# Group A attention: halo queries copied from wider q tiles, v stored by head group, one store for the halo outputs

## The chip, the cores and the metric

The kernel runs on one core of one Trainium2 chip. The metric is device time in microseconds for one launch; the program has float32 inputs and outputs. The engines are named as in the profile: PE (TensorE, matmul), PEld (its weight loads), DVE (VectorE), ACT (ScalarE), POOL (GpSimd) and SP (SyncE), which here only issues DMAs. A DMA that SP or ACT issues is followed by its queue: an engine issues its instructions in order, and an instruction whose wait is not over holds up those behind it.

## What is computed

One encoder layer with shared weights runs on two inputs, a prompt of 1024 tokens (sequence 0) and a sample of 512 tokens (sequence 1). Sixteen meta tokens are put before each, so n is 1040 and 528.

```python
n = rms_norm(x, g_mix)
qa, ka, va, qb, kb, vb = split(n @ w_in)
# group A: 8 query heads of 64, 2 key/value heads (4 query heads share one), per-head RMS norm of q and k, rotary
oa = softmax(qa @ ka.T * scale) @ va
# group B: 4 heads, each with two softmax maps, the second weighted by a learned lambda and subtracted
ob = rms_norm((softmax(q1 @ k1.T * scale) - lam * softmax(q2 @ k2.T * scale)) @ vb)
h = x + concat(oa, ob) @ w_out
# ConvGLU: depthwise convolution of width 3 over positions, GELU, gate
h = h + (gelu(conv3(rms_norm(h) @ w_gate)) * (rms_norm(h) @ w_up)) @ w_down
y = rms_norm(h)[16:]
```

The convolution of the first token that is returned (position 16) needs the row of position 15. Of the sixteen meta queries, position 15 alone is therefore computed: this is the halo.

## The kernel before

Matmuls that need float32 accuracy are done with a high part and a low part of each operand: `split` writes the high part on ACT and the rest on DVE or POOL, and `mm3` multiplies three times.

`projection` makes q, k and v for one sequence and stores them in DRAM. `pair` and `keys_a` write q and k as `qk` and `ka`; `values` writes v. For group A (`j == VA`) v in DRAM was `[128 tokens, n // 128 blocks, 256]`: for each token the high and low parts of key/value head 0 (128 columns), then those of head 1.

`attention` reads them back. For group A it loops over two key/value heads (`kv`), the four query heads of each (`i`), and blocks of 512 queries (`b`; two blocks for the prompt, one for the sample). `load_k` and `load_v` run once per `kv`; `load_q` runs once per block and loads two tiles `q0` and `q1` (high and low stacked in both orders) of 128 rows each, from a DRAM view whose outermost dimension is 4 (`stacked`). `softmax` does the scores of 128 queries on PE, scales on DVE (L405), and takes the exponential on ACT (L408). `reciprocals` sends 1/l through DRAM: it stores `rT`, and `load_r` reads it back broadcast as `o_rb`. `weighted_v` transposes p on PE, splits, and multiplies by v. `store_a` multiplies `o_a` by `o_rb` on POOL and stores to `oT`.

After the four heads of a `kv`, the halo queries are done: two columns (positions 14 and 15) of each of the four heads in two tiles, eight DMAs of 1 KB (L507), one small softmax, and four stores of one column each (L518).

Group B is `diff_block`: on POOL it computes `c` (L530) and adds the two maps (L532). Its q tiles (L559) are 306, 208 or 342 columns wide and use the same pool as group A's.

The work is staged in pairs. The sample's `projection` runs alone; then `merge` interleaves the sample's `attention` with the prompt's `projection`; then the prompt's `attention` with the sample's `mixer_out` and `conv_glu`; then the prompt's `mixer_out` and `conv_glu` run alone. `mixer_out` starts by loading `h` from `oT` (L612).

The program is written in this order, but the order on each engine is laid out when the program is built: the tile framework simulates the engines' time and puts the instructions of each queue in the order of that simulation (`schedule_with_timeline_sim=True`). A load whose source and buffer are free can so stand well ahead of the place where it is written. The halo tiles have two buffers, one for each `kv`.

Of the kernel before, what the change touches and what calls it, by code (L numbers as in the profile page):

```python
# [12 lines left out]
F32 = mybir.dt.float32  # L13
F32R = mybir.dt.float32r
# [6 lines left out]
P = 128  # L21
D = 1024
KT = D // P
NMETA = 16
HD = 64
# [10 lines left out]
QA, KA, VA, QB, KB, VB = 0, 4, 5, 6, 10, 14  # L36
# [120 lines left out]
def projection(ctx, g, s, side, tag, tag2):  # L157

    nc, tc = g.nc, g.tc
    n = SEQS[s] + NMETA  # L160
# [20 lines left out]
    with tc.tile_pool(name=f"ps{s}", bufs=2, side=side, reuse_waits="tile") as sp:  # L181
# [18 lines left out]
        c0, cw = chunks[0]  # L200
# [95 lines left out]
    def values(j):  # L296
        w = load_weight(g, g.w_in[j], lo_engine=nc.gpsimd)
        dst, tail = g.v[s][0 if j == VA else 1 + j - VB], g.vt[s][0 if j == VA else 1 + j - VB]
        for c0, cw in chunks:
            ps = g.psum.tile(P, cw, tag)  # L300
            dense(g, ps, w, xhi, xlo, c0, cw)
            t = bp.tile([P, cm], F32, name="t", tag="t", bufs=B1)[:, :cw]
            nc.vector.tensor_tensor(out=t, in0=ps, in1=rstd[:, c0:c0 + cw], op=ALU.mult)
            nt = -(-cw // P)
            v = bp.tile([P, 3, 2 * P], F32R, name="v", tag="v", bufs=2)
            ps = g.psum.tile(P, 512, tag2)
            for i in range(nt):
                kw = min(P, cw - i * P)
                nc.tensor.transpose(ps[:kw, i * P:(i + 1) * P], t[:, i * P:i * P + kw], g.ident)
            nf = cw // P  # L310
            for i0, i1, kw in ((0, nf, P), (nf, nt, cw - nf * P)):
                if i1 == i0:
                    continue
                pv = ps[:kw, i0 * P:i1 * P].rearrange("p (t c) -> p t c", c=P)
                if j == VA:
                    vv = v[:kw, i0:i1].rearrange("p t (m x c) -> p t m x c", m=2, x=2)
                    pv = pv.rearrange("p t (m c) -> p t m c", m=2)
                    hi, lo = vv[:, :, :, 0, :], vv[:, :, :, 1, :]
                else:
                    hi, lo = v[:kw, i0:i1, 0:P], v[:kw, i0:i1, P:2 * P]  # L320
                split(g, hi, lo, pv)
                t0 = c0 // P
                if kw == P:
                    nc.sync.dma_start(out=dst[:, t0 + i0:t0 + i1, :], in_=v.bitcast(F32)[:, i0:i1, :])
                    continue
                for r, part in ((16, 0), (48, 0)) if j == VA else ((16, 0), (48, 0), (80, 1)):
                    cc = slice(0, 2 * P) if j == VA else slice(part * P, (part + 1) * P)
                    nc.sync.dma_start(out=tail[r:r + kw, :cc.stop - cc.start], in_=v.bitcast(F32)[:kw, i0, cc])
            yield 25 * cw
# [19 lines left out]
def attention(ctx, g, s, side):  # L349
# [22 lines left out]
    def load_q(j, m, c0, cw):  # L372
        out = []
        for first in range(2):
            q = qp.tile([P, 512], F32R, name="q", tag=f"q{first}")[:, :cw]
            stacked(q, j, m, first, c0, cw)
            out.append(q)
        return out
# [6 lines left out]
        return k  # L385

    def load_v(i, w, c0):
        v = vp.tile([P, nf, 2 * P], F32R, name="v", tag="v")[:, :, :w]
        nc.sync.dma_start(out=v.bitcast(F32), in_=g.v[s][i][:, :, c0:c0 + w])
        tail = vp.tile([P, P], F32R, name="v_tail", tag="v_tail")[:64 if i == 0 else 96]  # L390
        nc.sync.dma_start(out=tail.bitcast(F32), in_=g.vt[s][i][:tail.shape[0], c0:c0 + P])
        return v, tail

    def softmax(q, k, l):

        M = q[0].shape[-1]
        p = pp.tile([P, ne], F32, name="p", tag="p")[:M]
        ps = g.psum.wide(M, nch, kw)
        for i in range(nch):
            kc = k[:, i * kw:(i + 1) * kw]  # L400
            nc.tensor.matmul(ps[:, i], lhsT=q[0], rhs=kc, start=True, stop=False)  # L401
            nc.tensor.matmul(ps[:, i], lhsT=q[1], rhs=kc, start=False, stop=True)  # L402

        nm = sp.tile([P, 1], F32, name="nm", tag="nm")[:M]
        nc.vector.tensor_scalar(out=p.rearrange("p (i w) -> p i w", i=nch), in0=ps, scalar1=-HD ** -0.5, scalar2=3.0e38,  # L405
                                op0=ALU.mult, op1=ALU.min, accum_out=nm)
        p = p[:, :n]
        nc.scalar.activation(p, p, AF.Exp, bias=nm, scale=-1.0, accum_out=l)  # L408
        return p
# [75 lines left out]
    for kv in range(2):  # L485
        k = load_k(KA, kv)
        v = load_v(0, P, kv * P)
        for i in range(4):
            h = kv * 4 + i
            for b in range(nblk):  # L490
                q = load_q(QA + 2 * kv, i, NMETA + 512 * b, 512)
                load_r()
                pl = []
                l = sp.tile([P, 4], F32, name="l_a", tag="l_a", bufs=3)
                for t in range(4):
                    pl.append(softmax([x[:, t * P:(t + 1) * P] for x in q], k, l[:, t:t + 1]))
                    yield 2 * n
                cols = slice(1 + 512 * b, 513 + 512 * b)
                reciprocals(l, g.rT[s][h, cols].rearrange("(t p) -> t p", p=P))
                o, W = yield from weighted_v(pl, v, False)  # L500
                oa = finish_a(o, W)
                store_a()
                late.append((oa, g.rT[s][h:h + 1, cols], g.oT[s][h * HD:(h + 1) * HD, cols]))
        halo = [sp.tile([P, 8], F32R, name="halo", tag=f"halo{f}", bufs=2) for f in range(2)]
        for i in range(4):
            for f in range(2):
                stacked(halo[f][:, 2 * i:2 * i + 2], QA + 2 * kv, i, f, NMETA - 2, 2)  # L507
        l = sp.tile([P, 4], F32, name="l_a", tag="l_a", bufs=3)[:8, 0:1]
        load_r()
        p = softmax(halo, k, l)  # L510
        r = sp.tile([P, 4], F32, name="r_a", tag="r_a", bufs=3)[:8, 0:1]
        nc.vector.reciprocal(out=r, in_=l)
        nc.scalar.activation(p, p, AF.Copy, scale=r)
        o, W = yield from weighted_v([p], v, False)
        oa = finish_a(o, W)
        for i in range(4):
            h = kv * 4 + i
            nc.sync.dma_start(out=g.oT[s][h * HD:(h + 1) * HD, 0:1], in_=oa[:, 2 * i + 1:2 * i + 2])  # L518
        store_a()

    def diff_block(qs, ks, v, cols):
        pl = []
        for c0, M in cols:
            l = sp.tile([P, 2], F32, name="l_b", tag="l_b")[:M]
            p0, p1 = [softmax([x[:, c0:c0 + M] for x in qs[m]], ks[m], l[:, m:m + 1]) for m in range(2)]
            r = sp.tile([P, 2], F32, name="r_b", tag="r_b")[:M]
            nc.vector.reciprocal(out=r, in_=l)
            nc.scalar.activation(p0, p0, AF.Copy, scale=r[:, 0:1])
            c = sp.tile([P, 1], F32, name="c", tag="c")[:M]
            nc.gpsimd.tensor_tensor(out=c, in0=r[:, 1:2], in1=g.neglam[:M], op=ALU.mult)  # L530
            nc.scalar.activation(p1, p1, AF.Copy, scale=c)  # L531
            nc.gpsimd.tensor_tensor(out=p0, in0=p0, in1=p1, op=ALU.add)  # L532
            pl.append(p0)
            yield 4 * n
        o, W = yield from weighted_v(pl, v, True)
        ob = op.tile([P, 512], F32, name="o_b", tag="o", bufs=3)[:, :W]
        nc.scalar.copy(ob, o)
        sq = op.tile([P, 512], F32, name="o_sq", tag="w1", bufs=1)[:, :W]
        nc.scalar.activation(sq, ob, AF.Square)
        ms = g.psum.tile(P, W, "o")  # L540
        nc.tensor.matmul(ms, lhsT=g.ones_v, rhs=sq, start=True, stop=True)
        rs = op.tile([P, 512], F32, name="o_rs", tag="w1", bufs=1)[:, :W]
        rsqrt_newton(g, op, rs, ms, W)
        nc.vector.scalar_tensor_tensor(out=ob, in0=ob, scalar=g.gsub, in1=rs, op0=ALU.mult, op1=ALU.mult)
        return ob
# [243 lines left out]
def trunk_kernel(ctx, tc, g):  # L789
# [5 lines left out]
    for s, N in enumerate(SEQS):  # L795
        n = N + NMETA
        g.qk.append([dram.tile([3, 2, P, n], F32, name=f"qk{s}_{i}") for i in range(len(PAIRS))])
        g.ka.append(dram.tile([2, 2, HD, n], F32, name=f"ka{s}"))
        g.v.append([dram.tile([P, n // P, 2 * P], F32, name=f"v{s}_{i}") for i in range(5)])

        g.vt.append(dram.tile([5, 96, 2 * P], F32, name=f"vt{s}"))
        g.oT.append(dram.tile([D, N + 1], F32, name=f"oT{s}"))
        g.rT.append(dram.tile([8, N + 1], F32, name=f"rT{s}"))
# [157 lines left out]
```

## Time and profile before

| | |
|---|---|
| median of 3 runs | 2271.11 us (2269.18 to 2272.93) |
| the profiled execution | 2271.76 us |
| its span, first to last instruction | 2270.0 us |
| mean granted TensorE clock | 0.967 |
| PE busy | 2139.6 us, 94% of the span |
| DVE, ACT, POOL busy | 56%, 46%, 29% |
| loads and stores of SP's queue | 115.82 MB in 85304 packets, 16.0% of the 16 DMA engines' span |
| halo loads | 32 of 1 KB |
| halo stores | 16 of 0.2 KB |

Busy time is that of one engine over the whole span; the share of a stretch can be far from it. A row of the timeline has a start and a duration in us, then engine, line, operation and tiles (`out<-in`); in brackets stands how long the engine had been idle, and what ended that. For SP the duration is the time in which it was held by the issue. A row of waits has who waited for whom, the total in us, the number of times, and the longest.

### The profile page before, as it was taken

Reading aid. Unit: us, or ns where it says so; the run is one execution under the profiler, and the core shown is the slowest. Engines: PE = TensorE matmul, PEld = TensorE weight load, DVE = VectorE, ACT = ScalarE, POOL = GpSimd, SP = SyncE. Lnnn points to the kernel's source line nnn. Section 1 sums busy time; section 2 is a strip of 40 time slices with the busy share of each in tenths; the row PEclk is TensorE's granted clock in tenths of the full one; section 3 lists DMA queues with packets and bytes.
Section 4 is the critical chain, followed back from the end, with each engine's and each line's share of the span. In section 5 each row is a group of like instructions: output and inputs, shape, how many; then the busy total and the mean of one; then the engine's idle time right before and its main releaser. Section 6 shows DMA issues by size and latency. Waiting matters only on the chain.

```text
span 2270.0 us, 32333 instructions
## 1 busy us (share of the span) xinstructions
PE 2139.6 (94%) x12442; PEld 1919.7 (85%) x12442; DVE 1272.2 (56%) x2203; ACT 1039.8 (46%) x1830; POOL 669.2 (29%) x514
## 2 busy tenths in 40 slices
PE   7887999986699999999999997999999999999997
PEld 6886999985598888888999996988888888888887
DVE  6635554454558667667777775774433444433446
ACT  5434554656547445466777775542122221122224
POOL 5862345531023212234444443431111001111005
PEclk8998999996899999999999998999999999999999
DMA  6573454443332232233323224631111111111112
GB/s 204 178 221 112 142 162 129 155 157 105 106 102 82 74 101 81 72 94 92 118 94 107 88 69 151 197 99 49 40 47 56 47 47 47 45 40 56 47 38 75
DMA packets 114259, 222.76 MB, mean 98 GB/s; under 512 B 16312, under 2 KB 67384, under 8 KB 113592
## 3 DMA queue, kind: packets, MB, share of 16 engines
q1 hardware_dynamic: 85304, 115.82, 16.0%
q10 hardware_dynamic: 28800, 104.87, 14.8%
q8 instruction: 98, 1.61, 0.3%
q14 instruction: 57, 0.47, 0.1%
HBM read 172.10 MB, written 48.55 MB: 97 GB/s over the span
## 4 chain that ended last, share of the span: by engine, by line
PE 81%; DMA 6%; DVE 5%; ACT 3%; issue 2%; POOL 1%; SPq 1%; DVEq 0%; ACTq 0%; POOLq 0%
PE ps_mm L129 20%; PE ps_mm L130 20%; PE ps_mm L131 20%; PE ps_t L422 5%; PE ps_s L401 3%; PE ps_s L402 3%; PE ps_o L437 2%; PE ps_o L436 1%; DMA q<-qk 1%; DMA v<-v 1%; PE ps_p L129 1%; PE ps_p L131 1%; PE ps_p L130 1%; PE ps_o L432 1%; DMA w_f<-w_out 1%
## 5 line engine op out<-in xcount | busy, mean ns | idle before, releaser
L129 PE MATMUL ps_mm<-xhi,w_hi 128*128 128x512 f32 (+6 forms) x1968 | 666.3, 339 | 0.7 <-ACT xhi L123 0.4
L130 PE MATMUL ps_mm<-xlo,w_hi 128*128 128x512 f32 (+6 forms) x1968 | 659.6, 335 | 0.6 <-POOL xlo L124 0.6
L131 PE MATMUL ps_mm<-xhi,w_lo 128*128 128x512 f32 (+6 forms) x1968 | 658.1, 334 | 0.0
L129 PEld LDWEIGHTS ps_mm<-xhi,w_hi 128*128 128x128 f32 x1968 | 373.7, 190 | 28.1 <-issue 1.7
L130 PEld LDWEIGHTS ps_mm<-xlo,w_hi 128*128 128x128 f32 x1968 | 373.8, 190 | 26.2 <-POOL xlo L124 1.3
L131 PEld LDWEIGHTS ps_mm<-xhi,w_lo 128*128 128x128 f32 x1968 | 373.3, 190 | 25.0 <-issue 0.5
L123 ACT CAST w_hi<-w_f 128x1024 fp32r<-128x1024 f32 x134 | 139.3, 1048 | 402.7 <-PE ps_mm L130 364.2
L405 DVE TENSOR_SCALAR_CACHE_REDUCE p<-ps_s 114x1044 f32<-114x1044 f32 (+5 forms) x212 | 223.4, 1054 | 127.7 <-PE ps_s L402 107.1
L124 POOL TENSOR_TENSOR a_lo<-gate,a_hi 128x512 fp32r<-128x512 f32 x66 | 99.4, 1507 | 660.3 <-ACT a_hi L123 659.3
L123 ACT CAST pt_hi<-ps_t 128x512 fp32r<-128x512 f32 (+6 forms) x360 | 168.9, 482 | 200.3 <-PE ps_t L422 169.7
L703 DVE TENSOR_TENSOR h<-ps_mm,h 128x512 f32<-128x512 f32 (+1 forms) x288 | 182.0, 644 | 121.8 <-PE ps_mm L131 121.1
L408 ACT ACTIVATE p<-p,nm 114x1040 f32<-114x1040 f32 (+5 forms) x212 | 215.2, 1015 | 74.0 <-DVE p L405 73.0
L124 DVE TENSOR_TENSOR pt_lo<-ps_t,pt_hi 128x512 fp32r<-128x512 f32 (+4 forms) x312 | 171.7, 564 | 125.5 <-ACT pt_hi L123 123.7
L130 PE MATMUL ps_mm<-a_lo,w_hi 128*128 128x512 f32 (+1 forms) x576 | 216.1, 378 | 0.0
L131 PE MATMUL ps_mm<-a_hi,w_lo 128*128 128x512 f32 (+1 forms) x576 | 216.1, 378 | 0.0
L129 PE MATMUL ps_mm<-a_hi,w_hi 128*128 128x512 f32 (+1 forms) x576 | 214.8, 385 | 0.4 <-DVE h L703 0.4
L401 PE MATMUL ps_s<-k,q 128*114 128x348 f32 (+4 forms) x552 | 180.8, 333 | 30.8 <-DMA q<-qk 16.9
L422 PE MATMUL ps_t<-ident,p 128*128 128x128 f32 (+7 forms) x1188 | 184.2, 270 | 2.4 <-ACT r_rows L457 2.0
L402 PE MATMUL ps_s<-k,q 128*114 128x348 f32 (+4 forms) x552 | 175.2, 323 | 4.4 <-DMA q<-qk 4.4
L124 DVE TENSOR_TENSOR w_lo<-w_f,w_hi 128x1024 fp32r<-128x1024 f32 x100 | 124.1, 1250 | 82.8 <-ACT w_hi L123 82.7
L422 PEld LDWEIGHTS ps_t<-ident,p 128*128 128x128 f32 (+7 forms) x1188 | 142.9, 136 | 31.7 <-issue 4.0
L532 POOL TENSOR_TENSOR p<-p 114x1040 f32<-114x1040 f32 (+2 forms) x56 | 115.0, 2053 | 128.9 <-ACT p L531 127.0
(189 smaller groups left out, 3547.2 us busy)
## 6 DMA issues: line engine op xcount, KB each, us to landing
w_f<-w_gate ACTq DMA_DIRECT2D x44, 512.0 KB
w_f<-w_up ACTq DMA_DIRECT2D x44, 512.0 KB
w_f<-w_down ACTq DMA_DIRECT2D x44, 512.0 KB
w_f<-w_in ACTq DMA_DIRECT2D x36, 512.0 KB
w_f<-w_out ACTq DMA_DIRECT2D x32, 512.0 KB
q<-qk SPq DMA_DIRECT2D x48, 256.0 KB
q<-qk SPq DMA_DIRECT2D x48, 171.0 KB
qk<-hi SPq DMA_DIRECT2D x20, 384.0 KB
```

The lines of the kernel that those rows point to most:

```text
L123: nc.scalar.copy(hi, src)
L124: (lo_engine or nc.vector).tensor_tensor(out=lo, in0=src, in1=hi.bitcast(F32), op=ALU.subtract)
L129: nc.tensor.matmul(ps, lhsT=whi, rhs=xhi, start=start, stop=False)
L130: nc.tensor.matmul(ps, lhsT=whi, rhs=xlo, start=False, stop=False)
L131: return nc.tensor.matmul(ps, lhsT=wlo, rhs=xhi, start=False, stop=stop).ins
L401: nc.tensor.matmul(ps[:, i], lhsT=q[0], rhs=kc, start=True, stop=False)
L402: nc.tensor.matmul(ps[:, i], lhsT=q[1], rhs=kc, start=False, stop=True)
L405: nc.vector.tensor_scalar(out=p.rearrange("p (i w) -> p i w", i=nch), in0=ps, scalar1=-HD ** -0.5, scalar2=3.0e38, op0=ALU.mult, op1=ALU.m ...
L408: nc.scalar.activation(p, p, AF.Exp, bias=nm, scale=-1.0, accum_out=l)
L422: nc.tensor.transpose(tps[:, c:c + M], p[:, k0:k0 + kw], g.ident[:M, :M])
L532: nc.gpsimd.tensor_tensor(out=p0, in0=p0, in1=p1, op=ALU.add)
L703: nc.vector.tensor_tensor(out=hs, in0=ps, in1=hs, op=ALU.add)
```

## The change

Group A's q tiles are 514 wide and start two columns earlier. At the first block of each head, the first two columns are copied by POOL into the halo tiles, which are now made before the loop over heads; the eight small loads are gone. The softmax of a block reads the columns from 2 on. Group A's v lies in DRAM as `[128, 2, n // 128, 128]`, so that what one key/value head reads is contiguous for a partition; its store is two DMAs for each chunk, and the v tile is contiguous too. The four halo stores of a `kv` are one DMA. To make room, the tiles `l_b` and `r_b` have six buffers instead of eight.

```diff
@@ values
                 if kw == P:
-                    nc.sync.dma_start(out=dst[:, t0 + i0:t0 + i1, :], in_=v.bitcast(F32)[:, i0:i1, :])
+                    part = v.bitcast(F32)[:, i0:i1, :]
+                    if j == VA:
+                        for m in range(2):
+                            nc.sync.dma_start(out=dst[:, m, t0 + i0:t0 + i1], in_=part[:, :, m * P:(m + 1) * P])
+                    else:
+                        nc.sync.dma_start(out=dst[:, t0 + i0:t0 + i1], in_=part)
                     continue
@@ attention, load_q and load_v
-            q = qp.tile([P, 512], F32R, name="q", tag=f"q{first}")[:, :cw]
+            q = qp.tile([P, 514], F32R, name="q", tag=f"q{first}")[:, :cw]
...
-        v = vp.tile([P, nf, 2 * P], F32R, name="v", tag="v")[:, :, :w]
-        nc.sync.dma_start(out=v.bitcast(F32), in_=g.v[s][i][:, :, c0:c0 + w])
+        v = vp.tile([P, nf * 2 * P], F32R, name="v", tag="v")[:, :nf * w].rearrange("p (t c) -> p t c", c=w)
+        nc.sync.dma_start(out=v.bitcast(F32), in_=g.v[s][0][:, c0 // P] if i == 0 else g.v[s][i])
@@ attention, group A
         v = load_v(0, P, kv * P)
+        halo = [sp.tile([P, 8], F32R, name="halo", tag=f"halo{f}", bufs=2) for f in range(2)]
         for i in range(4):
             h = kv * 4 + i
             for b in range(nblk):
-                q = load_q(QA + 2 * kv, i, NMETA + 512 * b, 512)
+                q = load_q(QA + 2 * kv, i, NMETA + 512 * b - 2, 514)
+                if b == 0:
+                    for f in range(2):
+                        nc.gpsimd.tensor_copy(halo[f][:, 2 * i:2 * i + 2], q[f][:, 0:2])
...
-                    pl.append(softmax([x[:, t * P:(t + 1) * P] for x in q], k, l[:, t:t + 1]))
+                    pl.append(softmax([x[:, 2 + t * P:2 + (t + 1) * P] for x in q], k, l[:, t:t + 1]))
...
-        halo = [sp.tile([P, 8], F32R, name="halo", tag=f"halo{f}", bufs=2) for f in range(2)]
-        for i in range(4):
-            for f in range(2):
-                stacked(halo[f][:, 2 * i:2 * i + 2], QA + 2 * kv, i, f, NMETA - 2, 2)
...
-        for i in range(4):
-            h = kv * 4 + i
-            nc.sync.dma_start(out=g.oT[s][h * HD:(h + 1) * HD, 0:1], in_=oa[:, 2 * i + 1:2 * i + 2])
+        nc.sync.dma_start(out=g.oT[s][kv * 4 * HD:(kv + 1) * 4 * HD, 0:1].rearrange("(i p) o -> p i o", p=HD),
+                          in_=oa.rearrange("p (i o) -> p i o", o=2)[:, :, 1:2])
@@ diff_block
-            l = sp.tile([P, 2], F32, name="l_b", tag="l_b")[:M]
+            l = sp.tile([P, 2], F32, name="l_b", tag="l_b", bufs=6)[:M]
...
-            r = sp.tile([P, 2], F32, name="r_b", tag="r_b")[:M]
+            r = sp.tile([P, 2], F32, name="r_b", tag="r_b", bufs=6)[:M]
@@ trunk_kernel
-        g.v.append([dram.tile([P, n // P, 2 * P], F32, name=f"v{s}_{i}") for i in range(5)])
+        g.v.append([dram.tile([P, 2, n // P, P] if i == 0 else [P, n // P, 2 * P], F32, name=f"v{s}_{i}")
+                    for i in range(5)])
```

## The prediction

> **What bounds the kernel now.** I read the page first (busy time, the chain that ended last), then busy time by stretch, then the waits and SP's queue where TensorE (PE) is idle.
>
> ```profile
> PE 2139.6 (94%) x12442; PEld 1919.7 (85%) x12442; DVE 1272.2 (56%) x2203; ACT 1039.8 (46%) x1830; POOL 669.2 (29%) x514
> ...
> PE 81%; DMA 6%; DVE 5%; ACT 3%; issue 2%; POOL 1%; SPq 1%; DVEq 0%; ACTq 0%; POOLq 0%
> ```
>
> PE is busy for 94% of the span, so time can only come from its gaps. By stretch (us; busy us of PE, PEld, DVE, ACT, POOL; clock; DMA share; GB/s):
>
> ```profile
> 150.00:205.00 55.00, 34.10 (x186) 30.73 (x185) 23.00 (x45) 19.67 (x39) 20.78 (x16) 0.78 0.48 146
> 205.00:490.00 285.00, 279.82 (x1806) 264.68 (x1805) 145.28 (x341) 151.56 (x330) 126.32 (x87) 0.99 0.44 145
> 490.00:600.00 110.00, 69.15 (x361) 57.80 (x359) 54.73 (x125) 59.65 (x135) 18.49 (x20) 0.75 0.44 131
> 600.00:700.00 100.00, 97.23 (x687) 88.06 (x685) 62.90 (x111) 55.01 (x105) 21.76 (x21) 0.99 0.32 89
> ```
>
> The changed transfers lie in attention, which begins for the sample near 157 and for the prompt near 505. Away from these two starts PE is 97 to 98% busy; from 490 to 600 it stands still for 40.9 us. The waits from 490 to 625:
>
> ```profile
> ACT xhi L123 <- DMA h<-oT: 15.5, 1, 15.5
> ...
> PE ps_o L446 <- DVE pt_hi L124: 14.9, 1, 14.9
> ...
> PE ps_s L401 <- DMA q<-qk: 13.3, 3, 5.0
> ...
> PE ps_s L402 <- DMA q<-qk: 2.9, 3, 1.1
> ```
>
> The first two are one stall: ScalarE (ACT) waits for `h`, DVE for ACT, PE for DVE. ACT's timeline shows its ends, DVE's when the last sample output `o_b` was made:
>
> ```profile
> 578.01 0.58 ACT L123 CAST pt_hi<-ps_t 128x512 fp32r<-128x512 f32 x1 [1.37 <-PE ps_t L422]
> 594.12 0.71 ACT L123 CAST xhi<-h 128x258 fp32r<-128x258 f32 x2 [15.52 <-DMA h<-oT]
> ```
>
> ```profile
> 573.67 0.53 DVE L544 SCALAR_TENSOR_TENSOR o_b<-o_b,gsub,o_rs 128x306 f32<-128x306 f32 x1
> ```
>
> `o_b` was ready at 573.67 + 0.53 = 574.2. SP's queue, which issues in order:
>
> ```profile
> 534.74 0.59 SPq L370 DMA_DIRECT2D q<-qk  x1
> 535.37 12.21 SPq L370 DMA_DIRECT2D halo<-qk  x8
> 547.62 1.06 SPq L370 DMA_DIRECT2D k<-ka  x2
> 548.72 0.56 SPq L389 DMA_DIRECT2D v<-v  x1
> ...
> 550.60 9.47 SPq L370 DMA_DIRECT2D halo<-qk  x6
> ...
> 560.63 1.08 SPq L370 DMA_DIRECT2D halo<-qk  x2
> 561.75 5.70 SPq L370 DMA_DIRECT2D k<-qk  x4
> 567.55 0.51 SPq L370 DMA_DIRECT2D q<-qk  x1
> 568.16 5.08 SPq L563 DMA_DIRECT2D oT<-o_b  x1
> ...
> 573.95 0.45 SPq L458 DMA_DIRECT2D rT<-r_rows  x1
> 582.20 0.49 SPq L474 DMA_DIRECT2D o_rb<-rT  x1
> 582.79 1.13 SPq L370 DMA_DIRECT2D q<-qk  x2
> 584.01 0.43 SPq L563 DMA_DIRECT2D oT<-o_b  x1
> 584.49 1.70 SPq L612 DMA_DIRECT2D h<-oT  x3
> ```
>
> The last `o_b` store left at 584.01, 9.8 us after its data were ready. SP was holding `o_rb`, which reads `rT` back, and `rT` took 582.20 - 573.95 = 8.25 us. `rT` itself was late: its rows were ready at 564.92 + 0.25 = 565.17, and SP reached it 8.8 us later, after k, q and sixteen halo loads.
>
> ```profile
> 564.92 0.25 ACT L457 COPY r_rows<-ps_t 4x128 f32<-4x128 f32 x1
> ```
>
> In a quiet place the same read-back starts 2.05 us after `rT`'s issue:
>
> ```profile
> 205.45 0.27 SPq L458 DMA_DIRECT2D rT<-r_rows  x1
> ...
> 207.50 0.50 SPq L474 DMA_DIRECT2D o_rb<-rT  x1
> ```
>
> **The change part by part, and the sum.** *Halo loads gone.* 32 loads leave SP, sixteen of them from the queue above: 12.21 + 9.47 + 1.08 = 22.8 us. That is not all gained: SP was also held back by loads in front. While q loads drained, the DMA moved this:
>
> ```profile
> 522.00:546.00 24.00, 14.28 (x52) 11.47 (x53) 6.77 (x20) 10.16 (x25) 2.43 (x4) 0.57 0.29 103
> ```
>
> Its issues by size (count, KB each):
>
> ```profile
> q<-qk SPq DMA_DIRECT2D x48, 256.0 KB
> ...
> k<-qk SPq DMA_DIRECT2D x8, 520.0 KB
> ```
>
> The share stayed at 0.29, about a quarter of the DMA engines, at 103 GB/s. So a 256 KB q load (262,144 B) takes 2.5 us and a 520 KB k load 5.2 us. If the earlier queue ends at 546, then `k<-ka` (5.2), v (512 KB on all engines, about 1.3 at four times that rate), two `k<-qk` (10.4) and two q loads (5.0) are through by about 568, without sixteen halos in between. `rT` can leave when ready, near 566, and lands by 566 + 2.05 = 568 at best, or, with the old lag of 8.25, at 574.3. The read-back and two q issues (0.49 + 1.13, with gaps 1.8 us in all, from 582.20 to 584.01) follow, so SP is free for the last `o_b` between 570 and 576.1. The store leaves between 574.2 (data) and 576.1, that is 7.9 to 9.8 us earlier. I take 9.0, nearer the data. `h` still needs 594.12 - 584.49 = 9.6 us, so it lands near 585, ACT still waits some 6 us from 578.6, and h stays what is late next. PE gets the 9.0 us back because from 600 on it is 97% busy. Ends for this step: 0 (SP's new order puts something slow ahead of the store again) and 14.9 (the PE wait goes altogether).
>
> The sixteen halo loads of the sample's start, and PE's longest wait there (150 to 230):
>
> ```profile
> L370 SPq DMA_DIRECT2D halo<-qk x16: 510/562/2470, 169.0 to 189.1; - x16
> ```
>
> ```profile
> PE ps_mm L232 <- POOL sq L228: 13.0, 1, 13.0
> ```
>
> PE waits there for POOL's work on a projection tile, and for no load; I take 0.
>
> *v by head group.* The prompt's group A v load goes from 512 B runs to 4 KB runs, the sample's from 512 B to 2 KB.
>
> ```profile
> 505.43 2.37 SPq L389 DMA_DIRECT2D v<-v  x1
> 507.85 8.37 SPq L391 DMA_DIRECT2D v_tail<-vt  x1
> ```
>
> SP held `v_tail` for 8.37 us behind it. But the q loads queued later still share a quarter of the engines with a k load (5.2 us) in front; sooner issue does not make that quarter faster. Bounds 0 and 8.4; I take 0.5, since the q waits have the k load before them in either case. The v stores become two for each chunk, five more DMAs on SP in the two projections, long before v is read: 0.
>
> *Halo copies on POOL.* 32 copies of 128x2. The nearest rows:
>
> ```profile
> L530 POOL TENSOR_TENSOR c<-r_b,neglam 114x1 f32<-114x1 f32 x36 | 15.0, 418 | 58.1 <-DVE r_b L527 58.0
> ...
> L530 POOL TENSOR_TENSOR c<-r_b,neglam 102x1 f32<-102x1 f32 x12 | 2.3, 194 | 32.1 <-DVE r_b L527 32.1
> ```
>
> At 0.19 to 0.42 us they are 6 to 13 us of an engine that is 29% busy: 0 on the path. The new wait is dearer than the copy: POOL now stands until a q load has landed, and behind it stand `c` and the sums of p (L530, L532), which PE's transposes wait for, and the projection's splits. A copy whose q landed long ago costs nothing; below nothing it cannot go. I take 0 and price the rest as a rival.
>
> The Trainium skill (SBUF — State Buffer, "Who interferes with whom") says that GpSimd shares a port pair with VectorE under an exclusive lock, and that a VectorE instruction with two SBUF inputs blocks against a GpSimd instruction that reads SBUF. By that rule each copy could hold VectorE for its own 0.19 to 0.42 us, an estimate of 13 us at most over all 32, and if PE waited for each, the time would be near 2275. The spread from 194 to 418 ns of an operation of one column agrees that small POOL work is sometimes held up; no row shows DVE paying for it.
>
> *Wider q, one output store, smaller pools.* Two more columns are 8 B on 2048 B, 0.4% of 2.5 us: 0. Four halo stores become one, four times, late in a stage where PE is busy: 0. Six buffers of `l_b` and `r_b` hold two blocks of three: 0.
>
> Sum: 9.0 + 0.5 = 9.5 us. The profiled execution took 2271.76, which is 0.65 above the median of 2271.11. 2271.76 - 9.5 = 2262.3, against the median 2261.6; I say 2262.
>
> **Rivals.** *The stall forms again (2271).* The order of each engine's instructions is laid out anew at build time. If POOL copies of the second head's q stand ahead of this `c`, they wait until the q loads issued by 534.74 are through, near 546:
>
> ```profile
> 538.39 0.19 POOL L530 TENSOR_TENSOR c<-r_b,neglam 102x1 f32<-102x1 f32 x1 [15.65 <-DVE r_b L527]
> ```
>
> The chain to `o_b` is then 546 - 538.4 = 7.6 us later, and of the 9.5 only 1.9 stay: 2269 to 2271. For it: POOL waits in order. Against it: POOL had stood idle 15.65 us there, and the copies could well stand behind.
>
> *More goes (2246).* With v and halos out of the way the three q waits (13.3 + 2.9 = 16.2 us) go too: 2262.3 - 16.2 = 2246. Against it: these q loads were issued before the halos, behind other q and k loads.
>
> *Slower (2280).* POOL's new waits reach PE in the merged stages, where POOL also makes the projection's low halves. Price: what a q load is late where it is late, 13.3 / 3 = 4.4 us. Of sixteen heads in both sequences, three such hits cost 13.2 and end at 2275.5, past +0.2% (4.5 us, about what this kernel's measurement can tell from no change); four cost 17.7 and give 2280. It decides from the third on. Against it: PE lost only 5.2 us in the whole stretch from 205 to 490, and q is loaded ahead there.
>
> **How the numbers follow.** Forecast (gain of 5 to 14 us, 2258 to 2267 its own range): 0.42. More goes: 0.12. Within 0.2%: 0.22, the re-formed stall and gains too small to tell. Slower: 0.24, the POOL waits, with a new order of PE at either start among them. Faster is 0.42 + 0.12 = 0.54. The range reaches to both outer cases, 2246 and 2280.
>
> **What would show it.** Right: no halo loads on SP; near 570 to 590 the last `oT<-o_b` leaves within 2 us of DVE's `o_b`; ACT's wait for `h` falls from 15.5 to about 6 us; PE's busy time is unchanged. Wrong: POOL rows of the copies with idle time ended by `DMA q<-qk`, followed by DVE, ACT or PE waiting for POOL; the wait for `h` still near 15 us; or a PE order at 500 to 600 with longer q waits.

## The result, and the profile after

The changed kernel takes 2274.38 us (median of 20 runs, 2266.82 to 2277.92) against 2270.75 us before (20 runs, 2266.41 to 2275.03): ratio 1.0017, 95% interval 1.0011 to 1.0023. It is 3.9 us slower, where 9.5 us faster was forecast. Below, a ratio is always that to the runs of the kernel before on the same chip, and "us" beside it is the ratio times 2270.

The profiled execution took 2269.86 us, 4.5 below its own median, while that of before took 2271.76, 1.0 above the median of its runs. These two traces therefore show where time moved, and not how much in all. Page of the changed kernel, busy time and the chain that ended last:

```profile
PE 2133.9 (94%) x12442; PEld 1911.6 (84%) x12442; DVE 1267.5 (56%) x2203; ACT 1040.2 (46%) x1830; POOL 676.0 (30%) x546
...
PE 81%; DMA 7%; DVE 5%; ACT 3%; issue 2%; POOL 2%; SPq 1%; ACTq 0%; DVEq 0%; POOLq 0%
```

The bound is the same. DMA and POOL each have one per cent more of the chain. By stretch, with the columns of the prediction's table:

```profile
205.00:490.00 285.00, 275.84 (x1777) 259.98 (x1776) 143.04 (x336) 148.47 (x325) 126.97 (x97) 0.99 0.44 143
490.00:600.00 110.00, 73.29 (x394) 60.54 (x392) 61.30 (x138) 66.37 (x148) 21.60 (x27) 0.81 0.42 139
600.00:700.00 100.00, 96.50 (x688) 87.51 (x689) 62.97 (x108) 53.78 (x102) 23.24 (x27) 1.00 0.29 84
```

From 490 to 600 PE is busy 4.1 us longer than before, so something was gained there. From 205 to 490 it is busy 4.0 us less: the merged stage of the sample, for which the prediction's sum has nothing, has lost. (The windows are fixed while the stages shift, so the sizes come further down.) SP's queue of the changed kernel:

```profile
508.35 1.77 SPq L396 DMA_DIRECT2D v_tail<-vt  x1
...
535.45 4.78 SPq L375 DMA_DIRECT2D k<-ka  x2
...
572.22 0.27 SPq L463 DMA_DIRECT2D rT<-r_rows  x1
573.14 0.53 SPq L375 DMA_DIRECT2D q<-qk  x1
573.76 0.50 SPq L479 DMA_DIRECT2D o_rb<-rT  x1
574.35 0.53 SPq L375 DMA_DIRECT2D q<-qk  x1
579.36 0.35 SPq L567 DMA_DIRECT2D oT<-o_b  x1
579.76 3.75 SPq L616 DMA_DIRECT2D h<-oT  x8
```

No halo load is left; `k<-ka` leaves 12.2 us earlier, and SP stands idle before the last store. But that store leaves only 4.65 us earlier than before (584.01), because its data are late:

```profile
578.80 0.54 DVE L548 SCALAR_TENSOR_TENSOR o_b<-o_b,gsub,o_rs 128x306 f32<-128x306 f32 x1
```

`o_b` is ready at 579.34, 5.1 us later than before (574.2). POOL's timeline says why:

```profile
529.60 0.19 POOL L500 CAST halo<-q 128x2 fp32r<-128x2 f32 x1 [8.22 <-PE ps_t L427]
532.16 0.19 POOL L500 CAST halo<-q 128x2 fp32r<-128x2 f32 x1 [2.37 <-DMA q<-qk]
532.30 1.30 POOL L536 TENSOR_TENSOR p<-p 104x528 f32<-104x528 f32 x1
543.35 0.19 POOL L500 CAST halo<-q 128x2 fp32r<-128x2 f32 x1 [9.76 <-DMA q<-qk]
546.79 0.19 POOL L500 CAST halo<-q 128x2 fp32r<-128x2 f32 x1 [3.25 <-DMA q<-qk]
546.93 0.19 POOL L534 TENSOR_TENSOR c<-r_b,neglam 102x1 f32<-102x1 f32 x1
```

The copies are 0.19 us each; the bracket is the price. Two stand ahead of the `c` that ran at 538.39 before, and it now runs at 546.93. The waits of the changed kernel from 490 to 625 show who stood behind it:

```profile
POOL halo L500 <- DMA q<-qk: 40.1, 5, 22.0
...
PE ps_s L406 <- DVE p L410: 14.5, 13, 7.6
...
DVE r_b L531 <- ACT p L413: 11.0, 3, 8.2
...
ACT p L535 <- POOL c L534: 7.7, 1, 7.7
...
PE ps_t L427 <- POOL p L536: 3.7, 1, 3.7
...
ACT xhi L123 <- DMA h<-oT: 1.5, 1, 1.5
```

From below: ACT's wait for `h` fell from 15.5 to 1.5 us. In exchange a `p` of ACT waited 7.7 us for `c`, the next exponential stood behind it in ACT's order, DVE waited 8.2 us for that one, and PE 7.6 us for DVE. Over the whole span the copies look like this (who ended POOL's idle time ahead of them, us and times):

```profile
L500 POOL CAST halo<-q x32: 186/186/772, 167.5 to 869.8; 128x2 fp32r<-128x2 f32 x32
...
  DMA q<-qk: 131.9, 31
```

31 of the 32 copies found their q not yet landed. They kept POOL 7.2 us busy, and POOL stood waiting for their loads for 131.9 us. The kernel lost far less than that, since POOL is idle anyway; three places show a loss.

**Three places.** Four rows of a timeline cut the run into stages: PE's first scores of the sample, the prompt's first `k<-ka`, the first `xhi<-h`, and the prompt's own `h`. For the kernel before (its `xhi` at 594.12 stands in the prediction), for the changed kernel, and for the variant `behind_v_store` (below), which has the whole change except that no q tile is wider, POOL copies nothing, and `l_b` and `r_b` keep eight buffers:

```profile
185.42 0.28 PE L401 MATMUL ps_s<-k,q 128*128 128x264 f32 x1
...
503.44 1.89 SPq L370 DMA_DIRECT2D k<-ka  x2
...
1373.13 3.75 SPq L612 DMA_DIRECT2D h<-oT  x7
```

```profile
183.04 0.28 PE L406 MATMUL ps_s<-k,q 128*128 128x264 f32 x1
...
503.92 3.32 SPq L375 DMA_DIRECT2D k<-ka  x2
...
584.51 1.33 ACT L123 CAST xhi<-h 128x258 fp32r<-128x258 f32 x4 [1.53 <-DMA h<-oT]
...
1370.59 4.03 SPq L616 DMA_DIRECT2D h<-oT  x7
```

```profile
183.08 0.28 PE L406 MATMUL ps_s<-k,q 128*128 128x264 f32 x1
...
498.21 3.10 SPq L375 DMA_DIRECT2D k<-ka  x2
...
571.72 0.72 ACT L123 CAST xhi<-h 128x258 fp32r<-128x258 f32 x2 [1.01 <-DMA h<-oT]
...
1352.44 3.93 SPq L617 DMA_DIRECT2D h<-oT  x7
```

Differences of neighbouring rows, with those of the other variants from the same rows of theirs (one profile each; kernels in which PE has the same order within a stage differ there by up to 3.7 us, as the changed kernel and `act_prompt` do in stage 1, so a difference of 2 us is little):

| kernel | halos: sample / prompt | 1: sample with projection | 2: hand-over | 3: prompt with mixer and GLU |
|---|---|---|---|---|
| before | DMA / DMA | 318.0 | 90.7 | 779.0 |
| changed | POOL / POOL | 320.9 | 80.6 | 786.1 |
| behind_v_store | DMA / DMA, late | 315.1 | 73.5 | 780.7 |
| halo_behind | DMA / DMA, late | 317.8 | 76.5 | 780.1 |
| copies_only | POOL / POOL | 322.9 | 81.1 | 786.6 |
| pool_behind | POOL / POOL, late | 321.4 | 74.6 | 787.3 |
| act_prompt | POOL / ACT | 324.6 | 75.3 | 780.8 |
| act_sample | ACT / POOL | 311.5 | 76.5 | 788.2 |
| late_act | ACT / ACT | 312.9 | 76.9 | 782.7 |
| act_behind | ACT / DMA, late | 311.4 | 76.6 | 780.7 |
| v_only | DMA / DMA | 316.2 | 85.2 | 780.9 |
| wide_only | DMA / DMA | 318.9 | 90.9 | 780.1 |
| store_only | DMA / DMA | 318.1 | 90.1 | 777.7 |
| act_spare | DMA / DMA | 319.8 | 89.3 | 779.8 |

With the sample's copies on POOL stage 1 takes 320.9 to 324.6, without 311.4 to 319.8; kernels with the same layout of v lie further apart (322.9 against 317.8 to 319.8 with the old one, 320.9 to 324.6 against 311.4 to 316.2 with the new). With the prompt's on POOL stage 3 takes 786.1 to 788.2, without 777.7 to 782.7. Against `behind_v_store` the changed kernel is longer by 5.8, 7.1 and 5.4 us: 18.2 of the 19.5 by which its profiled time is (2269.86 against 2250.34).

In stage 1 the wait looks like this, POOL's rows and then PE's:

```profile
295.30 0.19 POOL L500 CAST halo<-q 128x2 fp32r<-128x2 f32 x1 [4.91 <-DMA q<-qk]
298.96 0.19 POOL L500 CAST halo<-q 128x2 fp32r<-128x2 f32 x1 [3.48 <-DMA q<-qk]
299.10 1.00 POOL L228 TENSOR_TENSOR sq<-sq,eps 128x384 f32<-128x384 f32 x1
```

```profile
300.15 0.91 PE L232 MATMUL ps_mm<-sq,ones_four 128*128 128x384 f32 x2 [1.73 <-POOL sq L228]
```

and in stage 3, waits from 600 to 1380, then one of the places:

```profile
POOL halo L500 <- DMA q<-qk: 39.1, 10, 8.6
...
PE ps_mm L130 <- POOL xlo L124: 3.6, 3, 3.0
PE ps_mm L130 <- POOL a_lo L124: 1.9, 1, 1.9
```

```profile
723.98 0.19 POOL L500 CAST halo<-q 128x2 fp32r<-128x2 f32 x1 [2.61 <-DMA q<-qk]
724.12 1.32 POOL L124 TENSOR_TENSOR xlo<-t,xhi 128x256 fp32r<-128x256 f32 x2
```

```profile
724.81 0.39 PE L130 MATMUL ps_mm<-xlo,w_hi 128*128 128x258 f32 x1 [2.99 <-POOL xlo L124]
```

PE's two groups make 5.5 us (0.6 of that stood there before too, by the same view), about the 5.4 by which stage 3 is longer than in `behind_v_store`. In stage 1 the rows that name POOL make only 1.7 us of the 5.8; the rest is in q waits (3.9 + 2.0 against 3.6 + 1.5 before) and in many gaps too small to place.

### The profile page after: what moved, and what is told of

It reads as the page before. It is cut to its first block, busy times and chain, and to the rows that moved or that the text cites. A ratio compares the mean times of both kernels' runs of the same rounds, so it can differ in the third digit from the quotient of the medians.

```text
span 2268.1 us, 32318 instructions
## 1 busy us (share of the span) xinstructions
PE 2133.9 (94%) x12442; PEld 1911.6 (84%) x12442; DVE 1267.5 (56%) x2203; ACT 1040.2 (46%) x1830; POOL 676.0 (30%) x546
## 4 chain that ended last, share of the span: by engine, by line
PE 81%; DMA 7%; DVE 5%; ACT 3%; issue 2%; POOL 2%; SPq 1%; ACTq 0%; DVEq 0%; POOLq 0%
PE ps_mm L129 20%; PE ps_mm L130 20%; PE ps_mm L131 19%; PE ps_t L427 5%; PE ps_s L406 3%; PE ps_s L407 3%; DMA q<-qk 3%; PE ps_o L442 1%; PE ps_o L441 1%; PE ps_p L129 1%; PE ps_p L131 1%; PE ps_p L130 1%; DMA w_f<-w_out 1%; PE ps_o L437 1%; PE ps_o L438 1%
## 5 line engine op out<-in xcount | busy, mean ns | idle before, releaser
L695 DVE TENSOR_TENSOR gate<-ps_mm,gate 128x512 f32<-128x512 f32 x66 | 45.6, 691 | 191.2 <-PE ps_mm L131 188.4
```

The source lines that it names most:

```text
L695: nc.vector.tensor_tensor(out=a, in0=up, in1=a, op=ALU.mult)
```

## The experiments

Each kernel was timed 4 to 12 times. Theory A: the forecast gains are there, and POOL, standing in order for q loads, gives back more than all of them. It had three rivals, with letters in the expectations where they come up: the gain never existed, because something other than SP's halo loads set the hand-over; another part costs the time (v, the wider q, the store, the smaller pools); or what differs is the order that is laid out anew at each build.

**The halo loads alone: `halo_behind`.** The kernel before, with the prompt's 16 halo loads behind the sample's last `o_b` store on SP.

```diff
+        with tc.issue_after(g.last_store.ins) if s == 0 else nullcontext():
             for i in range(4):
                 for f in range(2):
                     stacked(halo[f][:, 2 * i:2 * i + 2], QA + 2 * kv, i, f, NMETA - 2, 2)
```

> The kernel before, with one thing moved: the prompt's sixteen halo loads stand on SP behind the sample's last store of o_b; q tiles, v and stores are as before, and PE's order is the same. Theory A (the halo loads held up SP, and through the read-back of rT the last o_b store and the load of h): ACT's wait for h falls from 15.5 us to 7 or less, the time falls by 7 to 10 us against before. Rival B (SP had no part in it, h is late for another reason): wait and time stay within 2 us of before.

Measured: 2258.15 us, ratio 0.9952 (0.9939 to 0.9964), -10.9 us, a little more than A's 7 to 10. ACT's first `xhi`, with its wait for `h` in the bracket:

```profile
578.47 0.72 ACT L123 CAST xhi<-h 128x258 fp32r<-128x258 f32 x2 [1.66 <-DMA h<-oT]
```

Up to that row PE, DVE and POOL have the order of before; on SP, besides the halo loads, one earlier store of `o_b` has changed places with the k loads. Not all of PE's order was kept, as the expectation had it: from 586 to 599 us 24 of its 12442 instructions stand elsewhere (by the sequences of operations and tiles in the two traces; so are the later counts). But the gain is made ahead of them (stage 2 is 14.2 us shorter, stage 3 is 1.1 longer), so it is SP's queue that was worth it. The step of the prediction that was put at 9.0 is worth 8 to 14.

**The prompt's copies of the first key/value head moved: `pool_behind`.** The changed kernel, these copies behind the sample's last sum of p; the order of PE, DVE and SP is that of the changed kernel throughout.

```diff
+                    with tc.issue_after(g.padd.ins) if s == 0 and kv == 0 else nullcontext():
                         for f in range(2):
                             nc.gpsimd.tensor_copy(halo[f][:, 2 * i:2 * i + 2], q[f][:, 0:2])
```

> The changed kernel, with one thing moved: the prompt's POOL halo copies of the first key/value head stand on POOL behind the last sum of the sample's two maps (p, L536), so no c and no p waits behind a copy there. PE's order is the same. Theory A (copies that wait for q loads hold c and p, and that eats what the freed SP queue gave): PE's waits of 7.6 us (DVE p) and 3.7 us (POOL p) near 530 to 550 go, the time falls by 7 to 11 us against the changed kernel, 3 to 8 us below before. Rival C (the loss lies in the changed order elsewhere): within 2 us of the changed kernel, 1 to 6 us above before.

Measured: 2266.50 us, 0.9993 (0.9984 to 1.0002), -1.6 against before and 5.5 less than the changed kernel. `c` runs early again and POOL's copies come after it:

```profile
539.79 0.19 POOL L535 TENSOR_TENSOR c<-r_b,neglam 102x1 f32<-102x1 f32 x1 [14.53 <-DVE r_b L532]
...
551.12 0.56 POOL L501 CAST halo<-q 128x2 fp32r<-128x2 f32 x4
```

Stage 2 shrank from 80.6 to 74.6, the other two stayed. With the orders of the other engines at the hand-over kept, the wait there is shown, and it costs about 6 us. The 5.5 us lie below A's 7 to 11 and above C's 2: the hand-over alone isn't the whole loss, as A in its first form had it.

**One part at a time.** `copies_only`: before with the wider q, the POOL copies and the six buffers. `v_only`: before with v by head group. `wide_only`: before with q 514 wide and the six buffers, halos by DMA. `store_only`: before with one halo store for each `kv`.

> One part of the change alone: wider q tiles and POOL halo copies, with the six buffers; v's layout and the four stores are as before. Theory A: the whole effect is here, 1 to 6 us above before, with PE waiting behind POOL near 530 to 550. Rival D (v's layout or the single store costs the time): within 2 us of before or below it.

> One part of the change alone: group A's v by head group in DRAM; halo loads and stores as before. Theory A: 0 to 2 us below before, v_tail no longer holds SP for 8 us at the prompt's start, and the q waits of PE there change by less than 2 us. Rival D: 3 us or more above before.

> Before with q tiles of 514 columns that start two columns earlier and six buffers for l_b and r_b; halos still loaded by DMA, nothing copied; PE's order is that of before. Theory A: within 2 us of before. Rival C (wider rows at another offset cost the loads more): 3 us or more above.

> Before with the four halo stores of a key/value head as one. Theory A: within 2 us of before. Rival D (the single store costs): 2 us or more above.

| kernel | median us | ratio | us |
|---|---|---|---|
| copies_only | 2272.09 | 1.0015 (1.0007 to 1.0024) | +3.4 |
| v_only | 2265.14 | 0.9982 (0.9973 to 0.9991) | -4.1 |
| wide_only | 2269.75 | 1.0004 (0.9996 to 1.0013) | +0.9 |
| store_only | 2268.15 | 0.9998 (0.9990 to 1.0007) | -0.5 |

No other part costs anything: the wider rows (with the order of PE, DVE, POOL and SP as before) and the one store are within what can be measured, and v gains more than the 0 to 2 us expected. The copies alone turn the 10.9 us that the missing loads bring into a loss: they cost about 3.4 + 10.9 - 0.9 = 13.4 us there, an estimate that takes the sample's missing loads for worth nothing.

`copies_only` also answers for stage 3. Outside stage 1, where 31 instructions moved, PE has the order of before to the last instruction, and stage 3 takes 786.6 us against 779.0. PE's waits for POOL from 600 to 1380 are those of the changed kernel:

```profile
PE ps_mm L130 <- POOL xlo L124: 3.5, 3, 2.9
PE ps_mm L130 <- POOL a_lo L124: 1.8, 1, 1.8
```

In `v_only` the wait for `h` is shorter, and SP's hold on `v_tail` is cut from 8.37 to 0.66 us:

```profile
505.67 0.66 SPq L396 DMA_DIRECT2D v_tail<-vt  x1
```

```profile
ACT xhi L123 <- DMA h<-oT: 12.4, 1, 12.4
```

**The other parts together: `behind_v_store`.** `halo_behind` with v by head group and the one store.

> No copies: halo loads as before, but the prompt's sixteen queued on SP behind the sample's last o_b store; with v by head group and one halo store. Theory A: the two gains add, 10.2 + 3.2, so 10 to 14 us below before. Rival E (v's gain and the freed queue are the same wait of ACT for h, so they do not add): 9 to 11 us below before.

Measured: 2251.17 us, 0.9925 (0.9913 to 0.9937), -17.0 us (14.3 to 19.7). The 10.9 and 4.1 of its parts make 15.0, inside that interval: they add, and E falls; A's 10 to 14 was too little. The changed kernel is this one with the wider q, six buffers and POOL copies in place of the late loads, and 17.0 + 3.9 = 20.9 us slower.

**The copies on another engine.** `late_act` is the changed kernel with all 32 copies on ACT, behind the fourth exponential of a head's first block: the scores before it have read that q, so the copy can't wait for it. `act_prompt` and `act_sample` move the prompt's or the sample's only and leave the other half on POOL.

```diff
-                if b == 0:
-                    for f in range(2):
-                        nc.gpsimd.tensor_copy(halo[f][:, 2 * i:2 * i + 2], q[f][:, 0:2])
...
+                    if b == 0 and t == 3:
+                        with tc.issue_after(g.exp.ins):
+                            for f in range(2):
+                                nc.scalar.copy(halo[f][:, 2 * i:2 * i + 2], q[f].bitcast(F32)[:, 0:2])
```

> The changed kernel with the halo copies taken off POOL: ACT makes them, queued behind the exponential of the fourth score tile of each head's first block, so that the q tile has landed when the copy's turn comes and no queue waits for a load because of a copy. Theory A (POOL's waits for q loads cost what the freed SP queue and v's layout gave): SP gives 10.2 us and v 3.2 us, both are kept, so 9 to 14 us below before; PE no longer waits for POOL's sq near 300, for p and c near 530 to 550, for xlo near 720. Rival C (wider q or the changed order costs it): within 4 us of before.

> The changed kernel with the prompt's sixteen copies on ACT behind the fourth exponential of the block, and the sample's sixteen still on POOL. Theory A (POOL's waits cost in three places: near 200 to 300 in the sample's attention, at the prompt's start near 530 to 550, and in the prompt's later heads near 690 to 720): the last two go, the first stays: 13 to 17 us below the changed kernel, 9 to 13 below before. Rival F (it is the prompt's start alone, as moved by 5.5 us before): 5 to 7 us below the changed kernel.

> The other half: the sample's sixteen copies on ACT behind the exponential, the prompt's still on POOL. Theory A: only the first of three places goes, 3 to 6 us below the changed kernel, within 3 us of before. Rival F: within 2 us of the changed kernel.

| kernel | median us | ratio | us against before | against the changed kernel |
|---|---|---|---|---|
| late_act | 2253.12 | 0.9932 (0.9920 to 0.9944) | -15.4 | -19.3 |
| act_prompt | 2263.78 | 0.9964 (0.9951 to 0.9978) | -8.2 | -12.1 |
| act_sample | 2255.33 | 0.9926 (0.9913 to 0.9938) | -16.8 | -20.7 |

With the same copies, of the same columns, where they can't wait, the kernel is within the intervals as fast as `behind_v_store` without any. But order and place changed together: against the changed kernel 1344 of PE's 12442 instructions stand elsewhere in `late_act`, 1146 in `act_sample`. `act_prompt` is cleaner: in stages 1 and 2 PE, DVE and SP keep the changed kernel's order, and stage 2 falls from 80.6 to 75.3, by what `pool_behind` also gave. The expectations of the halves were a miss: -12.1 and -20.7 don't add to -19.3, and `act_sample` gained several times what either theory gave; `late_act` gained more than its 9 to 14, `act_prompt` less than its 13 to 17. The stages show that the hand-over of `act_sample` shrank too (76.5 against 80.6), though its prompt's copies stayed on POOL. They still stand ahead of `c` there, but at other places, and ACT's waits for `c`, one of 7.7 us in the changed kernel, are now these (480 to 615):

```profile
ACT p L539 <- POOL c L538: 3.1, 3, 2.4
```

So a part of what `act_sample` gained may be the re-laid order; no run separates it.

**Order against waits: `act_behind` and `act_spare`.** The first has the sample's copies on ACT and the prompt's halos as late DMAs, with no POOL copy left; the second is `wide_only` with the sample's ACT copies, into a tile nobody reads.

```diff
+        spare = [sp.tile([P, 8], F32R, name="spare", tag=f"spare{f}", bufs=1) for f in range(2)]
...
+                    if s == 1 and b == 0 and t == 3:
+                        with tc.issue_after(g.exp.ins):
+                            for f in range(2):
+                                nc.scalar.copy(spare[f][:, 2 * i:2 * i + 2], q[f].bitcast(F32)[:, 0:2])
```

> The changed kernel, with the sample's halo copies done by ACT behind the fourth exponential of a head's first block, and the prompt's halos loaded by DMA again, sixteen small loads behind the sample's last o_b store; POOL copies nothing. Theory A (POOL's waits for q cost in the sample's merged stage, in the hand-over and in the prompt's merged stage; each is gone here, and h leaves early): the sample's stage as in the variant with ACT copies there (-16.8 against before), and of the 5 us by which the prompt's last stage is longer with POOL copies than without, all come back: -19 to -23 against before. Theory G (the gain of the sample's ACT copies is a re-laid order that happens to be good; another program lays another): anywhere from -10 to -17, with the first stage of 318 us not shortened to 311.

> The kernel before with q tiles 514 wide and, for the sample alone, the same ACT copies as in the variant above, but into a spare tile that nobody reads; the halos are loaded by DMA as before, v and the output stores are as before. Theory A (ACT copies gain only in that POOL's are gone): within 2 us of before. Theory G (eight copies behind the exponentials re-lay the order of the sample's stage, and that order is the gain): 5 to 9 us faster than before, with the first stage some 6 us shorter.

Measured: `act_behind` 2249.56 us, 0.9918 (0.9904 to 0.9931), -18.6; `act_spare` 2269.39 us, 1.0004 (0.9995 to 1.0013), +0.9. ACT copies by themselves bring nothing. That does not dispose of G: in `act_spare` only 4 of PE's instructions moved against before, so the order in question was not laid there. `act_behind` came 0.4 us short of A's span, with stage 1 at 311.4 as A had it and stage 3 back at 780.7; but in stage 1 PE has the very order of `act_sample`, so it doesn't test another one. It and `behind_v_store` are the fastest, with intervals that overlap. In `act_behind` a wait for `h` is left:

```profile
ACT xhi L123 <- DMA h<-oT: 12.6, 1, 12.6
```

**What stays open.** How the 20 us split between waits and order. Where PE's order was kept, the wait is shown: some 6 us at the hand-over (`pool_behind`, `act_prompt`), and stage 3 (`copies_only` against before). For stage 1 no run separates them. The three kernels with the sample's copies on ACT share one order of PE in stage 1, in which 833 instructions stand elsewhere than in `behind_v_store`; whether that order makes the 311.4 to 312.9 us against 315.1 was not tested.

## Why the prediction was wrong

- **Halo loads gone, 9.0: right.** `halo_behind` gave 10.9 (8.2 to 13.8). Counted from the prompt's first `k<-ka`, the last `o_b` store left 10.1 us earlier, a little more than the 7.9 to 9.8 of the working. It was off at one place, which makes the close number partly luck: `h` was to need 9.6 us after its issue and to stay late; it needed 578.47 - 574.07 = 4.4 us, with

```profile
574.07 4.87 SPq L613 DMA_DIRECT2D h<-oT  x8
```

- **v by head group, 0.5: too small.** 4.1 us (2.0 to 6.1), within the bounds of 0 to 8.4. I put v beside the q waits, which did stay as they were (13.1 + 3.0 us in `v_only`). The gain shows at the hand-over, whose length falls from 90.7 to 85.2: the last `o_b` store leaves 2.5 us earlier after the first `k<-ka`, and `h` needs 6.6 us instead of 9.6. How much of that is the 8.37 us hold of `v_tail`, which stands on SP ahead of the same queue, was not isolated; 85 of PE's instructions stand elsewhere there too.
- **Halo copies on POOL, 0: the step that failed.** It cost 13.4 us without v's change (`copies_only`) and about 20 with it (20.9 less the 0.9 of `wide_only`; what the re-laid order adds or takes is in both), more than all gains. On POOL the copies stood waiting for q, and `c`, `p`, `sq`, `xlo` and `a_lo` behind them came late to PE. The copy's own price was right (186 ns, 7.2 us in all). The sentence "a copy whose q landed long ago costs nothing" was true and had no case: 31 of 32 waited. q is loaded ahead of PE's use, as I said, but POOL has its copies ahead of that use too; what counts is how long q has landed when POOL reaches the copy, and I had no row for that.
- **Rivals.** "The stall forms again" named the place and the mechanism: `c` behind two copies, to run near 546 (546.93 by the trace), `o_b` 7.6 us later (5.1). "Slower" named the other two places, POOL's waits reaching PE in the merged stages. I priced them apart, as alternatives; they have one cause, a copy that waits in POOL's order, and came together. The price of 13.2 to 17.7 for three or four hits was near the 13 to 20 measured by luck: it counts hits of 4.4 us in the merged stages alone, where the rows show single PE waits of 1.7, 3.0 and 1.9 us. It was set against a gain of 9.5, which was itself 17.0. Three hits, 2275.5, were called past +0.2%, but that is 4.4 above 2271.11 and just within 4.5. By size the result, +0.17%, falls under "within 0.2%" (0.22). "More goes" fell: `behind_v_store` has neither early halos nor the slow v, and PE still waits for q:

```profile
PE ps_s L406 <- DMA q<-qk: 12.4, 3, 5.1
```

- **Wider q, one store, smaller pools, 0: right** (+0.9 and -0.5, both within their intervals of nothing).
- The Trainium skill (SBUF — State Buffer, "Who interferes with whom") has GpSimd and VectorE lock each other out of a shared port pair. Its sum of 2275 lies beside the measured 2274.4, and the trace gives it no support: with each copy holding VectorE for its own time, as the prediction took the rule, the lock could cost no more than the copies' measured 7.2 us, and `pool_behind`, which has as many POOL copies, is 5.5 us faster for having them later. No run here separates a remainder.

## What to carry to other kernels

An instruction on an in-order engine is priced by two rows: its own duration, and how long its operand has been there when the engine reaches it. Here 32 copies of 0.19 us, 31 of them of a tile still in flight, cost 13 to 20 us. When a transfer is replaced by a copy, put the copy behind something that has already waited for the same tile, or leave the transfer and move it out of the chain. And price rivals that share one cause together.

## What was not expected of the hardware

How long an issue holds SP went with the loads ahead of it. At the prompt's first key/value head `v_tail` held SP for 7.04 to 8.37 us in the six profiles with v in 512 B runs ahead of it, and for 0.66 to 1.77 us in the eight with the same bytes in 4 KB runs. The layout is not all of it: behind 512 B runs at the second head it was 1.23 us in the kernel before and 4.27 in `halo_behind`. And the load of `h` took 9.6, 4.4, 3.1 or 7.3 us from issue to its first use in four kernels (before, `halo_behind`, `behind_v_store`, `act_behind`); what made the difference was not isolated, but it is not a constant to be carried over.
